# Sample rows projected with the first group of prompt tiles, their attention placed behind its routing; staging buffer in two halves

## The chip, the cores and the metric

One core of a Trainium2 chip runs one launch of a Bass/Tile kernel. The metric is device microseconds of that launch, as a median of a few executions. Arithmetic is float32 throughout; in the last stage float32 operands are split in a high and a low part. Instructions run on five engines, each in its own fixed order: PE (matrix products), DVE (vector), ACT (scalar, activations), POOL (here only the indirect row gathers) and SP (issues nearly all other transfers). The order on each engine is decided when the program is built, by the Tile framework's scheduler from its own estimates; at run time nothing overtakes.

## The reference, cut

One layer of a hybrid decoder for 1024 prompt rows and 8 sample rows with the same weights:

```python
h = rmsnorm(x) * (1 + sc1) + sh1
qa, ka, va, ub, vb, xr, xg = split(h @ w_in)            # 1024 -> 2560 columns
ya = dilated attention(q, k, v)       # sample rows: against their cache of 512 rows and themselves
yb = spatial_gate(ub, rmsnorm(vb));   yc = rglru_block(xr, xg)
x = x + g1 * ([rms(ya) | rms(yb) | rms(yc)] @ w_out)
x = x + g2 * peer_ffn(rmsnorm(x) * (1 + sc2) + sh2)
def peer_ffn(h):                      # 8 heads, 16 experts each, of 16384
    q = rmsnorm(h @ w_q); s = q . sub_keys              # 2 x 128 scores a head
    e, g = top 16 of the sums of the two top-16 lists;  g = softmax
    act = gelu(h . u_tab[e]);  return sum over k of (g * act)_k v_tab[e_k]
def dilated_attn_sample(q, k_all, v_all):   # three branches, merged by their denominators
    logits = q . k_all[idx] * scale + bias;  out = softmax(logits) . v_all[idx]
```

## The kernel before, in words

The prompt is eight tiles of 128 rows; the eight sample rows are tile `NT`. The kernel has a **front** and a **last stage**, and a **gather stream** runs beside both.

The front goes over `GROUPS` = (0,1), (2,3), (4,5,NT), (6,7). For each group `project` loads the five 512-column blocks of `w_in` (L86, four transfers a block, a ring of four buffers) and forms q, k, v and the two other mixers; `mix_and_route` does the attention of its prompt tiles (L605 scores, L622 values), for `NT` calls `sample_attention`, then multiplies by `w_out` (into L696), normalises, multiplies by `w_q`, and takes the top-16 lists. `select` turns these into 128 expert numbers and gates a row. A product of a prompt tile is eight matmuls (L237); of `NT` it is eight narrow ones and a summing one (L241, L245).

Tiles 1, 3, 4, 5 (`DENSE`) are later multiplied with all 16384 experts, and for that `gate_table` writes their gates as a table to HBM: per step DVE makes one-hot rows (L796), four matmuls go to the single buffer `psG` (L804), and ACT copies it to `st` (L805); every fourth step one 1 MB transfer writes `st` out (L806, `g_d<-st`). `st` has one buffer. The steps are fed into the program between attention heads (`pump`).

Tiles 0, 2, 6, 7 (`GATHER`) and at last `NT` go through the gather stream (`experts`): POOL fetches 128 rows of `peer_u`, one a partition, 512 KB a time (L893), DVE forms the dot product (L901), 128 times; then the same with `peer_v` and a weighted sum (L910). Tiles follow each other strictly: 256 gathers, then L917 and L918 finish the tile, its output leaves, and the next tile's rows are loaded into the same buffer `gx`. `NT` needs 8 + 8 gathers. The ring `grow` has five buffers, so POOL runs at most five gathers ahead of DVE.

The last stage `dense` starts when all gate tables are written: 128 blocks of `peer_u` and `peer_v` are loaded and split (L969), multiplied (L999 scores, L1015 values), and added up on DVE (L1024); it ends with L1043 and L1044 for each dense tile.

`sample_attention` takes for each of the 8 sequences the row q (`qb`), two blocks of cached keys (`kc`: 128 and 96 rows), multiplies and sums on DVE (L824, L825), forms the softmax, and multiplies with two blocks of cached values each (`vc`, L868, 16 matmuls into one `psv`). Its tiles come from the routing stream's ring `R.a2`, four buffers; two of them hold the weights `pz` while the values come in.

Of the kernel before, what the change touches and what calls it, by code (L numbers as in the profile page):

```python
# [21 lines left out]
D = 1024  # L22
NT = 8
GATHER = (0, 2, 6, 7)
DENSE = (1, 3, 4, 5)
GROUPS = ((0, 1), (2, 3), (4, 5, NT), (6, 7))
# [33 lines left out]
def kernel(ctx: ExitStack, tc: tile.TileContext, I, O):  # L60
# [12 lines left out]
    class Stream:  # L73


        def __init__(self, key, weights, rows):
            self.key, self.weights, self.rows = key, weights, rows
# [4 lines left out]
        def load_w(self, src):  # L82
            ws = []
            for j in range(4):
                w = fr.tile([P, 2, 512], F32, tag="w" + self.key, name="w", bufs=self.weights)
# [13 lines left out]
    Z = Stream("z", 4, 4)  # L99
    R = Stream("r", 4, 4)  # L100
# [435 lines left out]
    qT, mix = {}, {}  # L536

    def project(grp):
# [7 lines left out]
        for nb in (4, 0, 1, 3, 2):  # L546
            w = Z.load_w(I["w_in"][nb])
            for t in grp:
# [79 lines left out]
    def mix_and_route(grp, first):  # L628
        if first:
            ada(R, "g1")  # L630
        pt = [t for t in grp if t < NT]
        sums = {t: sm.tile([P, 8], F32, tag="sums", name="sums", bufs=4) for t in pt}
# [20 lines left out]
        if NT in grp:  # L653
            sample_attention(mix[NT])
# [131 lines left out]

    def gate_table(t):
# [3 lines left out]
        for b in range(P // TB):  # L791
            st = fr.tile([P, P, TB], F32, tag="st", name="st", bufs=1)
            for n0 in range(0, TB, 4):
# [5 lines left out]
                ps = mm.tile([P, 512], F32, tag="pg", name="psG", bufs=BANKS["g"])  # L799
                for q in range(4):  # L800
# [9 lines left out]
    def sample_attention(mix):  # L810
# [7 lines left out]
        for b in range(8):  # L818
            qb = R.a2("qb")
            S.dma_start(qb, dram_ap(q_d, b * 512, [[0, P], [1, 512]]))  # L820
            for j, (r0, st, n) in enumerate(blk):
                kc = R.a2("kc")
# [3 lines left out]
        kn = R.a2("kn")[:8]  # L826
        S.dma_start(kn, k_d)
        qs = R.a2("qs2")[:8]
# [5 lines left out]
        lg = R.a2("lgs")[:64, :225]  # L834
# [5 lines left out]
        ohs = R.a2("ohs")[:33, :225]  # L840
# [16 lines left out]
        for j, n in ((0, P), (1, 96)):  # L857
            z = R.a2("pz").rearrange("p (b c) -> p b c", b=8)
# [4 lines left out]
        po = R.ps("psv")  # L863
        for b in range(8):
            for j, (r0, st, n) in enumerate(blk):
                vc = R.a2("vc")
# [7 lines left out]
        om = R.a2("om")[:64]  # L874
# [6 lines left out]
        tv_ = R.a2("tv")[:8]  # L881
# [3 lines left out]
        V.tensor_tensor(mix[:8, 0:512], tv_, py[:8], op=ALU.add)  # L885
# [290 lines left out]
```

## Time and profile before

| | us |
|---|---|
| median of 3 runs | 3316.39 (3306.85 to 3317.27) |
| profiled execution, whole | 3327.76 |
| its span, first to last instruction | 3326.0 |
| busy in the span: PE / DVE / POOL / ACT | 2795.2 / 2543.4 / 1394.1 / 1201.9 |

The profiled execution is 0.3% over the median, so sums are made against its span and carried over as a ratio. The busy shares are averages over stages of different kinds: the front (to about 1707 us), the last stage (to about 3314 us) and a short end.

### The profile page before, as it was taken

The numbers are of one execution on the slowest core, as the hardware profiler recorded it, in microseconds if no ns is written. First come the engines' busy times: TensorE is split into PE (matmuls) and PEld (weight loads), VectorE is DVE, ScalarE is ACT, GpSimd is POOL, SyncE is SP. The second block draws the span as 40 slices with busy tenths as digits, with TensorE's granted clock in tenths as the row PEclk, the third lists the DMA queues.
The fourth block names the chain that finished last, engine by engine and source line by source line (L and its number), as shares of the span: only waits on it lengthen the run. The fifth ranks groups of instructions, "written<-read, shape, count | busy, mean of one in ns | idle before, by whom it ended". The sixth has DMA issues, their size and how long they took to land.

```text
span 3326.0 us, 35751 instructions
## 1 busy us (share of the span) xinstructions
PE 2795.2 (84%) x11152; PEld 1879.5 (57%) x11152; DVE 2543.4 (76%) x5342; ACT 1201.9 (36%) x2583; POOL 1394.1 (42%) x1046
## 2 busy tenths in 40 slices
PE   7999976868944888976759998988989988989997
PEld 2444353423630333554437777777777776777776
DVE  1324876896675777876799898788898888898896
ACT  2453474443630342664543222222222222222221
POOL 0000043414235532034323565466566656566563
PEclk8999997987955999987879999999999999999998
DMA  7556677947787987478887999899999999999996
GB/s 276 179 195 198 217 250 269 335 170 287 221 253 247 352 261 285 139 229 296 276 287 252 347 333 334 301 345 339 348 329 342 344 344 342 360 332 333 346 347 218
DMA packets 340157, 952.56 MB, mean 286 GB/s; under 512 B 35063, under 2 KB 117550, under 8 KB 337918
## 3 DMA queue, kind: packets, MB, share of 16 engines
q0 software_dynamic: 149760, 545.33, 46.6%
q1 hardware_dynamic: 190206, 404.95, 35.1%
q8 instruction: 88, 1.44, 0.2%
q14 instruction: 103, 0.84, 0.1%
HBM read 894.04 MB, written 60.85 MB: 287 GB/s over the span
## 4 chain that ended last, share of the span: by engine, by line
PE 27%; DMA 23%; issue 20%; POOL 14%; DVE 12%; ACT 3%; SPq 0%; POOLq 0%; DVEq 0%; ACTq 0%
POOL grow L893 14%; PE psz L237 10%; DMA grow<-in_peer_v,ge 8%; DMA g_d<-st 5%; PE psG L804 3%; DVE grow L901 3%; DMA grow<-in_peer_u,ge 2%; PE pst L162 2%; PE pso L622 2%; PE psS L999 2%; PE psO L1015 2%; PE lg L605 2%; PE psa L194 2%; DVE acc L910 1%; DMA w<-in_w_in 1%
## 5 line engine op out<-in xcount | busy, mean ns | idle before, releaser
L893 POOL DMA_INDIRECT grow<-in_peer_u,ge x520 | 685.2, 1318 | 1333.2 <-DVE grow L901 540.5
L893 POOL DMA_INDIRECT grow<-in_peer_v,ge x520 | 708.3, 1362 | 565.7 <-DVE acc L910 359.2
L910 DVE SCALAR_TENSOR_TENSOR acc<-grow,dot,acc 128x1024 f32<-128x1024 f32 x515 | 660.1, 1282 | 136.6 <-DMA grow<-in_peer_v,ge 129.5
L237 PE MATMUL psz<-w,hT 128*128 128x512 f32 x1408 | 682.7, 617 | 59.4 <-DMA w<-in_w_in 28.4
L901 DVE SCALAR_TENSOR_TENSOR grow<-grow,gx 128x1024 f32<-128x1024 f32 x520 | 625.8, 1219 | 133.5 <-DMA grow<-in_peer_u,ge 108.9
L237 PEld LDWEIGHTS psz<-w,hT 128*128 128x128 f32 x1408 | 253.2, 196 | 324.1 <-issue 223.0
L1015 PE MATMUL psO<-vh,ah 128*128 128x512 f32 x512 | 223.2, 436 | 120.8 <-DVE acc L1024 120.3
L804 PE MATMUL psG<-o,oh 128*128 128x128 f32 x1024 | 205.8, 339 | 121.0 <-ACT st L805 113.3
L968 ACT CAST vh<-v 128x1024 fp32r<-128x1024 f32 x128 | 125.2, 1048 | 492.5 <-PE psO L1015 491.1
L804 PEld LDWEIGHTS psG<-o,oh 128*128 128x128 f32 x1024 | 170.9, 232 | 208.7 <-ACT st L805 147.8
L796 DVE TENSOR_TENSOR oh<-iof,tr 128x1024 f32<-128x1024 f32 x128 | 156.5, 1224 | 134.2 <-PE psG L804 129.5
L968 ACT CAST ah<-a 128x512 fp32r<-128x512 f32 x128 | 79.6, 622 | 398.0 <-DVE a L1004 398.0
L968 ACT CAST uh<-u 128x1024 fp32r<-128x1024 f32 x128 | 135.1, 1055 | 236.6 <-PE psS L999 236.4
L1015 PE MATMUL psO<-vl,ah 128*128 128x512 f32 x512 | 216.9, 424 | 0.0
L1015 PE MATMUL psO<-vh,al 128*128 128x512 f32 x512 | 215.2, 420 | 0.0
L803 ACT ACTIVATE o<-oh,tr 128x128 f32<-128x128 f32 x512 | 185.5, 397 | 53.2 <-PE psG L804 44.0
L1015 PE MATMUL psK<-vh,al 128*128 128x512 f32 x512 | 199.9, 391 | 5.0 <-DVE al L969 5.0
L1015 PE MATMUL psK<-vh,ah 128*128 128x512 f32 x512 | 200.0, 391 | 2.3 <-ACT ah L968 2.3
L1015 PE MATMUL psK<-vl,ah 128*128 128x512 f32 x512 | 199.8, 390 | 0.0
L1015 PEld LDWEIGHTS psO<-vh,ah 128*128 128x128 f32 x512 | 107.2, 209 | 159.8 <-DVE acc L1024 136.3
L969 DVE TENSOR_TENSOR ul<-u,uh 128x1024 fp32r<-128x1024 f32 x128 | 156.1, 1220 | 5.5 <-ACT uh L968 5.5
L969 DVE TENSOR_TENSOR vl<-v,vh 128x1024 fp32r<-128x1024 f32 x128 | 150.6, 1219 | 0.5 <-ACT vh L968 0.4
(370 smaller groups left out, 5002.8 us busy)
## 6 DMA issues: line engine op xcount, KB each, us to landing
u<-in_peer_uT SPq DMA_DIRECT2D x128, 512.0 KB
v<-in_peer_v SPq DMA_DIRECT2D x128, 512.0 KB
w<-in_w_in SPq DMA_DIRECT2D x80, 512.0 KB
w<-in_wq SPq DMA_DIRECT2D x64, 512.0 KB
g_d<-st SPq DMA_DIRECT2D x32, 1024.0 KB
gc<-g_d SPq DMA_DIRECT2D x16, 2048.0 KB
w<-in_w_ada SPq DMA_DIRECT2D x48, 512.0 KB
w<-in_w_out SPq DMA_DIRECT2D x32, 512.0 KB
```

What stands on the lines that cost most here:

```text
L162: T.transpose(pv[:, c, :r], src[:, (c0 + c) * P:(c0 + c + 1) * P], ident[:r, :r])
L194: T.matmul(ps[32 * j:32 * j + 32, :], sc[:, 2 * j + kk, :], w(2 * j + kk), start=(kk == 0), stop=(kk == 1 and j > 0))
L237: T.matmul(ps, xT[:, c, :], w(c), start=(c == 0), stop=(c == 7))
L796: V.tensor_tensor(oh, iof[:, None, None, :].to_broadcast([P, 2, OHB, P]), tt[:, 0:2, b * TB + n0:b * TB + n0 + OHB, None].to_broadcast([P, ...
L803: A.activation(o1, oh[:, 0, n0 % OHB + q, :], AF.Copy, scale=tt[:, 2, n:n + 1])
L804: T.matmul(ps[:, q * P:(q + 1) * P], oh[:, 1, n0 % OHB + q, :], o1, start=True, stop=True)
L893: G.indirect_dma_start(out=rt, out_offset=None, in_=tab, in_offset=bass.IndirectOffsetOnAxis(ap=idx, axis=0))
L901: V.scalar_tensor_tensor(rt, rt, 1.0, x, op0=ALU.mult, op1=ALU.mult, accum_out=w[:, k:k + 1])
L910: V.scalar_tensor_tensor(acc, rt, w[:, k:k + 1], acc, op0=ALU.mult, op1=ALU.add)
L968: A.copy(hi, x)
L969: eng.tensor_tensor(lo, x, hi, op=ALU.subtract)
L1015: T.matmul(ps, aa[x][:, t * P:(t + 1) * P], vv[y][:, hf * 512:(hf + 1) * 512], start=(k == 0 and (first or o not in keep)), stop=(k == 3 * ...
```

## The change

The sample rows move from the third group to the first one in `project` (`PROJECT`), and to the second one in `mix_and_route` (`GROUPS`). `sample_attention` stands by itself, right behind the routing of the first group; it hands its result over by a small HBM tensor `mix_d`. Its tiles no longer come from `R.a2` but from the buffers of the gate table: alternately `st`, which is now two halves with two buffers, and `oh12` (class `Early`). Its value product takes the buffer of `psG`. `gate_table` copies each step in two halves and writes two 512 KB transfers. `select` of a gather tile follows its routing at once, where it came after the next group's projection; `select(NT)` keeps that place. The modulation row `g2` is formed one group later.

```diff
-GROUPS = ((0, 1), (2, 3), (4, 5, NT), (6, 7))
+PROJECT = ((0, 1, NT), (2, 3), (4, 5), (6, 7))
+GROUPS = ((0, 1), (2, 3, NT), (4, 5), (6, 7))
...
+    class Early:
+
+        n = 0
+
+        def a2(self, name):
+            self.n += 1
+            shape, tag = (([P, P // 2, TB], "st"), ([P, 2, OHB, P], "oh12"))[self.n % 2]
+            x = fr.tile(shape, F32, tag=tag, name=name, bufs=2)
...
+        if NT in grp:
+            S.dma_start(mix_d[:, 512:1024], mix.pop(NT)[:8, 512:1024])
...
+        if NT in grp:
+            mix[NT] = fr.tile([P, D], F32, tag="mix", name="mix", bufs=4)
+            S.dma_start(mix[NT][:8], mix_d)
...
-        if NT in grp:
-            sample_attention(mix[NT])
...
-            st = fr.tile([P, P, TB], F32, tag="st", name="st", bufs=1)
+            sts = [fr.tile([P, P // 2, TB], F32, tag="st", name="st", bufs=2) for _ in range(2)]
...
-                A.copy(st[:, :, n0:n0 + 4], ps.rearrange("p (n c) -> p c n", n=4))
-            S.dma_start(g_d[:, :, j * (P // TB) + b, :, :].rearrange("g p c n -> p g (c n)"),
-                        st.rearrange("p (g c) n -> p g (c n)", c=GST))
+                for st, pv in zip(sts, ps.rearrange("p (n two c) -> two p c n", n=4, two=2)):
+                    A.copy(st[:, :, n0:n0 + 4], pv)
+            hg = P // GST // 2
+            for m, st in enumerate(sts):
+                S.dma_start(g_d[m * hg:(m + 1) * hg, :, j * (P // TB) + b, :, :].rearrange("g p c n -> p g (c n)"),
+                            st.rearrange("p (g c) n -> p g (c n)", c=GST))
...
-            qb = R.a2("qb")
+            qb = X.a2("qb")
...
-        po = R.ps("psv")
+        po = gate_ps("psv")
...
-        V.tensor_tensor(mix[:8, 0:512], tv_, py[:8], op=ALU.add)
+        V.tensor_tensor(tv_, tv_, py[:8], op=ALU.add)
+        S.dma_start(mix_d[:, 0:512], tv_)
...
     for i, grp in enumerate(GROUPS):
-        project(grp)
+        project(PROJECT[i])
         while late:
             now(select(late.pop()))
         mix_and_route(grp, i == 0)
...
             if t in DENSE:
                 pending += [select(t), gate_table(t)]
+            elif t == NT:
+                late.append(t)
             else:
-                late.append(t)
+                now(select(t))
         if i == 0:
+            sample_attention()
+        if i == 1:
             ada(R, "g2")
```

The order on the engines moves as follows. On PE, the sample attention (`psl`, `psb`, `psv`) of before stands between the last gate-table matmuls of the third group's attention and that group's first transposes of `mix`, with nothing of other work between its rows:

```order
L804 MATMUL psG<-o_6088,oh_6076 128x128
L837 MATMUL psl<-ident,lgT_6299 64x128
L838 MATMUL psl<-ident,lgT_6300 64x96
L843 MATMUL psb<-ohs,rb 64x225
L855 MATMUL psl<-ident,lgs 128x64
L856 MATMUL psl<-ident,lgs 96x64
L868 MATMUL psv<-vc,pz 64x512 x16
L878 MATMUL psv<-om,bm 8x512
L162 MATMUL pst<-ident,mix 128x128 x16
```

In the changed kernel (its own line numbers: L249 is the product `psz`, L174 a transpose, L493 a mixer) the same rows stand in the projection of the second group, a part of them is shown:

```order
L859 MATMUL psl<-ident,lgT_2324 64x128
L860 MATMUL psl<-ident,lgT_2325 64x96
L249 MATMUL psz<-w,hT 128x512
L865 MATMUL psb<-ohs,rb 64x225
L249 MATMUL psz<-w,hT 128x512 x12
L877 MATMUL psl<-ident,lgs 128x64
L878 MATMUL psl<-ident,lgs 96x64
L249 MATMUL psz<-w,hT 128x512 x4
L890 MATMUL psv<-vc,pz 64x512 x2
L174 MATMUL pst<-ident,z 128x128 x4
L890 MATMUL psv<-vc,pz 64x512 x2
L249 MATMUL psz<-w,hT 128x512 x2
```

Between the first and the last of the 16 value products (`psv`) stand now 17 products of the second group's projection and 8 transposes, which do not depend on them. On SP, the projection of the first group loads its weights (`w<-in_w_in`) like this in the kernel before:

```order
L86 DMA w<-in_w_in 128x1024 x6
L580 DMA out_k_p<-z 128x512
L583 DMA kT_d<-kt 128x4x128
L86 DMA w<-in_w_in 128x1024 x2
L580 DMA out_k_p<-z 128x512
L583 DMA kT_d<-kt 128x4x128
L640 DMA kT<-kT_d 128x256
L86 DMA w<-in_w_in 128x1024 x4
```

and in the changed kernel (L87 is the weights, L842 and L845 are the queries and cached keys of the sample rows) like this:

```order
L581 DMA q_d<-z 8x512
L842 DMA qb<-q_d 128x512
L845 DMA kc<-in_cache_k 96x512
L842 DMA qb<-q_d 128x512
L593 DMA out_k_p<-z 128x512
L845 DMA kc<-in_cache_k 96x512
L596 DMA kT_d<-kt 128x4x128
L845 DMA kc<-in_cache_k 128x512
L842 DMA qb<-q_d 128x512
L87 DMA w<-in_w_in 128x1024 x3
L593 DMA out_k_p<-z 128x512
L596 DMA kT_d<-kt 128x4x128
```

The weights now stand behind sample loads, each of which needs a free one of four buffers. On DVE, the program ends like this before (L910 with `dot` is the last gathers of the sample rows, L1024 to L1044 the end of the last stage, L947 the last step of the sample rows):

```order
L910 SCALAR_TENSOR_TENSOR acc<-grow,dot,acc 128x1024
L1044 TENSOR_TENSOR x1f<-x1f,tmp 128x1024
L1024 TENSOR_TENSOR acc_10713<-acc_10713,psO 128x512
L1043 TENSOR_TENSOR tmp<-grw,acc_10713 128x512
...
L1024 TENSOR_TENSOR acc_10716<-acc_10716,psO 128x512
L1043 TENSOR_TENSOR tmp<-grw,acc_10716 128x512
L1044 TENSOR_TENSOR x1f<-x1f,tmp 128x1024
L947 TENSOR_REDUCE fin<-part 128x64
```

and like this in the changed kernel, whose L933, L924 and L1067 are L910, L901 and L1044 of before:

```order
L933 SCALAR_TENSOR_TENSOR acc<-grow,dot,acc 128x1024
L1067 TENSOR_TENSOR x1f<-x1f,tmp 128x1024
L933 SCALAR_TENSOR_TENSOR acc<-grow,dot,acc 128x1024 x19
L940 TENSOR_TENSOR acc<-acc,grw 128x1024
L941 TENSOR_TENSOR acc<-acc,x1f 128x1024
L924 SCALAR_TENSOR_TENSOR grow,dot<-grow,gx 128x1024 x8
L926 TENSOR_TENSOR dot<-dot,gw 128x8
L931 TENSOR_SCALAR acc<-grow,dot 128x1024
L933 SCALAR_TENSOR_TENSOR acc<-grow,dot,acc 128x1024 x7
L973 TENSOR_REDUCE fin<-part 128x64
```

Behind the last row of the last stage stand now 19 sums of tile 7 and all of the sample rows' experts. Counted over DVE's whole order, 372 of the 1040 gather rows (L901, L908, L910) stand ahead of the first split of the last stage before, and 323 in the changed kernel; between that split and the last row L1044 there are 668 before, and 682 in the changed kernel. Apart from these 49 rows, what stands ahead of the last stage is the same set of instructions on PE and DVE; ACT has 128 copies of `st` and 7 table loads more there, SP 35 transfers more.

## Rows read from the trace of the kernel before

**Rows 1.** Busy time by stretch: stretch, its length, busy us (count) by engine.

```profile
core 0: us, PE busy (x) PEld busy (x) DVE busy (x) ACT busy (x) POOL busy (x), PEclk, DMA share, GB/s
0.00:396.00 396.00, 369.05 (x1210) 156.87 (x1210) 156.47 (x788) 158.90 (x407) 0.63 (x6) 0.97 0.63 211
396.00:767.00 371.00, 279.12 (x1081) 152.38 (x1081) 292.98 (x964) 196.24 (x498) 130.99 (x103) 0.86 0.73 252
767.00:976.00 209.00, 158.82 (x683) 102.72 (x679) 141.68 (x238) 111.74 (x275) 70.86 (x55) 0.74 0.80 259
976.00:1082.00 106.00, 34.66 (x42) 5.58 (x42) 63.95 (x75) 9.51 (x43) 56.70 (x41) 0.52 0.81 251
...
1707.00:3314.00 1607.00, 1456.59 (x6144) 1186.90 (x6144) 1397.45 (x1801) 420.69 (x537) 914.28 (x663) 0.95 0.91 329
3314.00:3326.00 12.00, 0.00 (x0) 0.00 (x0) 2.32 (x4) 0.00 (x0) 0.00 (x0) 0.56 0.34 85
```

**Rows 2.** PE's timeline, sample attention: start, length, what, idle and releaser.

```profile
974.04 2.08 PE L804 MATMUL psG<-o,oh 128*128 128x128 f32 x8 [0.68 <-ACT st L805]
...
1081.84 1.97 PE L162 MATMUL pst<-ident,mix 128*128 128x128 f32 x8 [8.10 <-ACT mix L669]
```

**Rows 3.** Who waited for whom, 976 to 1084 us: total us, times, longest.

```profile
ACT junk L666 <- PE psv L868: 62.1, 1, 62.1
```

**Rows 4.** Chain of waits, first and last transfer of cached values: start, length.

```profile
1016.40 8.25 DMA vc<-in_cache_v
...
1066.39 2.64 DMA vc<-in_cache_v
```

**Rows 5.** Groups of PE instructions, 60 to 396 us (each product is recorded as two).

```profile
L237 PE MATMUL psz<-w,hT 128*128 128x512 f32 x507 | 234.5, 602 | 5.3 <-DMA w<-in_w_in 4.8 <-DVE hT L327 0.5
```

**Rows 6.** What SP's queue waited for, 900 to 1085 us.

```profile
SPq L867 <- PE psv L868: 24.1, 13, 2.1
SPq L823 <- DVE lgT L825: 24.1, 7, 10.1
SPq L867 <- DMA vc<-in_cache_v: 18.8, 9, 5.9
```

**Rows 7.** ACT copies from PSUM (ns min/median/max), table loads in one stretch.

```profile
L805 ACT COPY st<-psG x128: 563/586/595, 425.1 to 1657.1; 128x512 f32<-128x512 f32 x128
...
L534 ACT COPY mix<-psy x8: 373/377/378, 87.0 to 1223.0; 128x256 f32<-128x256 f32 x8
...
L148 ACT ACT_TABLE_LOAD x4 | 5.1, 1283 | 0.1
```

**Rows 8.** Who waited for whom, whole span.

```profile
POOL grow L893 <- issue: 159.1, 520, 0.9
PEld psG L804 <- ACT st L805: 147.8, 81, 10.6
...
ACT st L805 <- DMA g_d<-st: 114.9, 24, 16.0
```

**Rows 9.** The page's costliest groups, the gather stream's: busy, mean ns | idle before.

```profile
L893 POOL DMA_INDIRECT grow<-in_peer_v,ge x520 | 708.3, 1362 | 565.7 <-DVE acc L910 359.2
L910 DVE SCALAR_TENSOR_TENSOR acc<-grow,dot,acc 128x1024 f32<-128x1024 f32 x515 | 660.1, 1282 | 136.6 <-DMA grow<-in_peer_v,ge 129.5
...
L901 DVE SCALAR_TENSOR_TENSOR grow<-grow,gx 128x1024 f32<-128x1024 f32 x520 | 625.8, 1219 | 133.5 <-DMA grow<-in_peer_u,ge 108.9
```

**Rows 10.** Timeline of DVE near the end.

```profile
3269.15 1.23 DVE L901 SCALAR_TENSOR_TENSOR grow<-grow,gx 128x1024 f32<-128x1024 f32 x1 [7.21 <-DMA gx<-h_d]
...
3301.06 1.28 DVE L910 SCALAR_TENSOR_TENSOR acc<-grow,dot,acc 128x1024 f32<-128x1024 f32 x1
...
3312.78 1.23 DVE L1044 TENSOR_TENSOR x1f<-x1f,tmp 128x1024 f32<-128x1024 f32 x1
```

**Rows 11.** Chain of waits behind the end of tile 7.

```profile
3256.66 5.92 DMA out_xp<-acc
3262.59 6.46 DMA gx<-h_d
```

More of the change, by code (lines that the diff above doesn't have):

```diff
@@ L73, with __init__ @@
     class Stream:
-        def __init__(self, key, weights, rows):
-            self.key, self.weights, self.rows = key, weights, rows
+        def __init__(self, key, rows):
+            self.key, self.rows = key, rows
         def ps(self, name="ps", kind="s"):
@@ L84, in load_w @@
             for j in range(4):
-                w = fr.tile([P, 2, 512], F32, tag="w" + self.key, name="w", bufs=self.weights)
+                w = fr.tile([P, 2, 512], F32, tag="w" + self.key, name="w", bufs=4)
                 S.dma_start(w, src[j])
@@ L97, in small @@
             return sm.tile([P, n], F32, tag=f"{nm}{n}{self.key}", name=nm, bufs=bufs)
-    Z = Stream("z", 4, 4)
-    R = Stream("r", 4, 4)
+    Z = Stream("z", 4)
+    R = Stream("r", 4)
+    class Early:
[4 more added lines that the diff above has]
+            x = fr.tile(shape, F32, tag=tag, name=name, bufs=2)
+            return x.rearrange("p a b -> p (a b)")[:, :512] if tag == "st" else x.rearrange("p a b c -> p (a b c)")[:, :512]
+    X = Early()
     def a4(name):
@@ L536 @@
     qT, mix = {}, {}
+    mix_d = dpool.tile([8, D], F32, name="mix_d")
     def project(grp):
@@ L785, in select, with gate_ps @@
         A.copy(tr[t], ps[:, :3 * P].rearrange("p (q n) -> p q n", q=3))
+    def gate_ps(name):
+        return mm.tile([P, 512], F32, tag="pg", name=name, bufs=BANKS["g"])
     def gate_table(t):
@@ L798, in gate_table @@
                                     op=ALU.is_equal)
-                ps = mm.tile([P, 512], F32, tag="pg", name="psG", bufs=BANKS["g"])
+                ps = gate_ps("psG")
                 for q in range(4):
@@ L804, in gate_table, with sample_attention @@
                     T.matmul(ps[:, q * P:(q + 1) * P], oh[:, 1, n0 % OHB + q, :], o1, start=True, stop=True)
-                A.copy(st[:, :, n0:n0 + 4], ps.rearrange("p (n c) -> p c n", n=4))
-            S.dma_start(g_d[:, :, j * (P // TB) + b, :, :].rearrange("g p c n -> p g (c n)"),
-                        st.rearrange("p (g c) n -> p g (c n)", c=GST))
+                for st, pv in zip(sts, ps.rearrange("p (n two c) -> two p c n", n=4, two=2)):
[4 more added lines that the diff above has]
+                            st.rearrange("p (g c) n -> p g (c n)", c=GST))
             yield
-    def sample_attention(mix):
+    def sample_attention():
         n_d = dpool.tile([8, 8], F32, name="n_d")
@@ L818, in sample_attention @@
         for b in range(8):
-            qb = R.a2("qb")
+            qb = X.a2("qb")
             S.dma_start(qb, dram_ap(q_d, b * 512, [[0, P], [1, 512]]))
             for j, (r0, st, n) in enumerate(blk):
-                kc = R.a2("kc")
+                kc = X.a2("kc")
                 S.dma_start(kc[:n], dram_ap(I["cache_k"], (b * 512 + r0) * 512, [[512 * st, n], [1, 512]]))
@@ L825, in sample_attention @@
                 V.tensor_reduce(lgT[j][:n, b, :], kc[:n].rearrange("p (h e) -> p h e", h=8), axis=AX.X, op=ALU.add)
-        kn = R.a2("kn")[:8]
+        kn = X.a2("kn")[:8]
         S.dma_start(kn, k_d)
-        qs = R.a2("qs2")[:8]
+        qs = X.a2("qs2")[:8]
         S.dma_start(qs, q_d)
@@ L833, in sample_attention @@
         S.dma_start(n_d, ln)
-        lg = R.a2("lgs")[:64, :225]
+        lg = X.a2("lgs")[:64, :225]
         S.dma_start(lg[:, 224:225], dram_ap(n_d, 0, [[1, 64], [1, 1]]))
@@ L839, in sample_attention @@
         A.copy(lg[:, 0:224], ps[:64, 0:224])
-        ohs = R.a2("ohs")[:33, :225]
+        ohs = X.a2("ohs")[:33, :225]
         S.dma_start(ohs, I["ohs"])
@@ L857, in sample_attention @@
         for j, n in ((0, P), (1, 96)):
-            z = R.a2("pz").rearrange("p (b c) -> p b c", b=8)
+            z = X.a2("pz").rearrange("p (b c) -> p b c", b=8)
             V.memset(z, 0.0)
@@ L862, in sample_attention @@
             pz.append(z)
-        po = R.ps("psv")
+        po = gate_ps("psv")
         for b in range(8):
             for j, (r0, st, n) in enumerate(blk):
-                vc = R.a2("vc")
+                vc = X.a2("vc")
                 S.dma_start(vc[:n], dram_ap(I["cache_v"], (b * 512 + r0) * 512, [[512 * st, n], [1, 512]]))
@@ L873, in sample_attention @@
         V.tensor_reduce(bm, ident[:64, :64].rearrange("p (b h) -> p b h", b=8), axis=AX.X, op=ALU.add)
-        om = R.a2("om")[:64]
+        om = X.a2("om")[:64]
         V.tensor_tensor(om.rearrange("p (h e) -> p h e", h=8), po[:64].rearrange("p (h e) -> p h e", h=8),
@@ L880, in sample_attention @@
         S.dma_start(pn, dram_ap(p_d, 0, [[8, 8], [1, 8]]))
-        tv_ = R.a2("tv")[:8]
+        tv_ = X.a2("tv")[:8]
         S.dma_start(tv_, v_d)
```

## Prediction

> **What bounds the kernel now.** I first cut the span into its stages. The front lasts to 1707 us, the last stage from there to 3314 us, and 12 us follow [rows 1]. In the last stage everything is near full at once: in 1607 us PE is busy 1457, DVE 1397, and the transfer engines 0.91 of the time. No single engine is the bound there, and the order on DVE, in which the dense work and the gather stream are woven together, fixes the pace. The first 396 us are PE's: busy 369 of 396 at a granted clock of 0.97, with DVE at 156. In between lies one stretch in which PE does almost nothing: from 976 to 1082 us it is busy 34.7 of 106 us, at a clock of 0.52 [rows 1]. That is the sample attention. The timeline of PE shows it between the last gate-table matmul and the first transpose of `mix` [rows 2], and the waits name who stands still: ACT waits 62.1 us in one piece for `psv`, since the norm of `mix` of the group stands behind it [rows 3]. The gather stream goes on meanwhile (POOL busy 56.7 of the 106 us), so that the stretch is dead for the front but not for the whole kernel. This is the point on which the forecast turns.
>
> **The change part by part.** The work is conserved, as the counts in the section on the change say, so I follow the idle time of PE through the front, and then the end.
>
> *The dead stretch goes.* It has 106 − 34.7 = 71 us without PE, and the sample products in it ran at a granted clock of 0.52. Where they stand now the clock was 0.97 [rows 1], about its upper level (2.4 GHz) instead of the lower one (1.2), so 34.7 us become some 18. Together −88 us in the front.
>
> *What waits where the sample rows stand now.* The 16 loads of cached values took from 1016 to 1069 us, 53 us [rows 4], with two free buffers, as now. Between the first and the last of their products stand now 17 products of 0.93 us (two records of 234.5/507 us, [rows 5]), 16 of the sample rows at the same price, and a few small ones: some 35 us of cover. If the loads keep their pace, 18 us are bare; without gathers beside them (POOL has none before 396 us, [rows 1]) they should be quicker. The other place is SP. The queries and keys stand ahead of weights, and SP stops at each that has no free buffer. In the present kernel SP waited 24.1 + 24.1 + 18.8 us for such buffers and values [rows 6]. The weight ring hides part: when one of the four tiles comes free, three are still to be used, 3 x 4 x 0.93 = 11 us of products for two prompt tiles. I take +15 us for both, from 0 (all covered) to 67 (every SP wait becomes a wait of PE). Queued behind them are the projections of the first two groups, and with these the start of the gathers.
>
> *The staging in halves.* A copy of 512 columns takes 586 ns, one of 256 from PSUM 377 [rows 7]; two are 168 ns dearer, 21.5 us for 128 steps. It is on the path where PE waits for the copy, 81 of the 128 steps [rows 8]: +14 us (0 to 22). The 7 more table loads of 1.28 us [rows 7] are 9 us on an engine that is busy 36%: +3 (0 to 9). The wait for the transfer itself, 114.9 us in 24 pieces [rows 8], I leave as it is: both halves are sent behind the last of the four steps, and `psG` has one buffer, so the next matmuls wait until the second half has landed too.
>
> *Less gather work in the front.* 49 dot products of 1.22 us [rows 9], 60 us of DVE, move out of the front. Some of them were what the front waited for; I take −15 us (0 to −60).
>
> *Early select.* Nothing for tile 2: its gathers follow those of tile 0 on POOL, and by 976 us, in the third group's attention, only 103 + 55 of tile 0's 256 were issued [rows 1]. Nothing for tile 0 either, as long as its lists come no earlier; the longer first part rather delays them.
>
> So the last stage starts at −88 + 15 + 14 + 3 − 15 = **−71 us**.
>
> *The last stage* has 682 gather rows beside it instead of 668: 14 × 1.28 us = 18 us of DVE [rows 9], of which I count half, since DVE is busy 87% of the time there (0 to 18). In exchange the change of buffers from tile 7 to the sample rows leaves it, which now stops DVE for 7.2 us [rows 10] and holds rows of the last blocks behind it: −10 (0 to −20). Together −1.
>
> *The end* pays. Before, the last dense row ended at 3314 us [rows 10] and only 12 us followed [rows 1]. Now 19 sums of tile 7 and the whole of the sample rows' experts follow. Up to four gathers are there already (4 × 1.28 us), the other 15 come at POOL's own pace of 1.36 + 0.31 us between two [rows 8, 9]: 30 us. Finishing the tile takes two DVE rows (2.4), its output and the next `gx` 5.9 + 6.5 us [rows 11], eight dot products 9.8, eight sums 10.3, and what came behind the last sum took from 3302 to 3326 us [rows 10]; without dense transfers ahead of it on SP I take 20 of these 24. Sum 85 us against 12: **+73 us** (60 to 90).
>
> Total: −71 − 1 + 73 = +1, so 3327 us on the span, 3326 × 1.0003. In the scale of the runs shown (the profiled span is 0.3% over their median): 3317, rounded to **3316 us**. The dead stretch is worth its 88 us to the front, and nearly the same is given back, because the gathers that filled it now stand alone at the end.
>
> **The rivals.** *B, the front gains more (faster).* The dots that leave the front count in full (60 instead of 15 us), or a step may start when the first half of `st` is out, which would save up to half of the 114.9 us [rows 8], 57 us. Either gives 3327 − 45 to 3327 − 57 = 3270 to 3282 on the span, 3260 to 3272 in the runs' scale. For it: DVE was busy 293 of 371 us between 396 and 767 us [rows 1]. Against the half: the single buffer `psG`. A rule of the Trainium skill (Perfetto Trace Analysis, DMA Optimizations) speaks for the half: splitting a transfer into smaller ones may let the whole end sooner where the transfer engines are mostly idle. Another one of the Trainium skill (DMA: Bandwidth & Descriptors, Rules for kernel authors) speaks against it: for bandwidth it wants 1 MiB or more in a DMA, and it calls two transfers to disjoint partition halves (here they are halves of the columns) not worth it, because they serialize. The trace has only whole transfers here, so no run shows which holds; the sum stays as it is by the second and would be 57 us lower by the first.
>
> *C, SP holds the weights back (slower).* Every wait of SP for a sample buffer reaches PE, 67 us instead of 15: 3327 + 52 = 3379 on the span, 3369 in the runs' scale. It decides from the point where the waits exceed the 11 us that the ring hides per block. For it: in the shown piece of SP's order three weight tiles stand behind eight sample and output transfers. Against: PE waited only 4.8 us for weights between 60 and 396 us [rows 5], and the transfer engines were busy only 0.63 of that time [rows 1].
>
> *D, no effect at all beyond the order*: the gather stream, the one chain that runs through front and last stage, keeps its mean pace whatever stands beside it, and the time changes only with its start. It starts as now, or 18 + 15 = 33 us later behind the longer first part: 3326 to 3359 on the span, 3316 to 3349 in the runs' scale.
>
> **How the numbers follow.** A measurement of this kernel can tell about 0.3%, 10 us, from no change. A, the sum, has 0.46; its own spread is about ±25 us (3291 to 3341), of which a half lies within 10 us: 0.12 faster, 0.22 same, 0.12 slower. B has 0.27, C 0.19, D 0.08 (0.02 faster, 0.02 same, 0.04 slower). Faster 0.12 + 0.27 + 0.02 = 0.41; same 0.24; slower 0.12 + 0.19 + 0.04 = 0.35. The range reaches half way and more into B and C: 3266 to 3362.
>
> **What would show it.** In the profile after: no stretch with PE under 40% between 400 and 1600 us; the first split of the last stage (the x rows of L969's successor) at about 1636 us; the last L1044's successor 71 or 72 us earlier than 3314, and some 85 us behind it in which PE is idle. Copies of `st` of about 377 ns, the waits for `g_d` unchanged near 115 us. C would show as waits of PE for `w<-in_w_in` well over 5 us before 400 us; B as a front below 1600 us. The prediction is wrong at its root if the last stage does not keep its 1607 us.

## The result, and the profile after

The changed kernel takes 3289.76 us (median), the one before 3316.83 us beside it: a ratio of 0.9898, with a 95% interval of 0.9856 to 0.994. One execution of the changed kernel took 5677 us, and is left out. A second comparison, beside the experiments, gave 0.9912 (0.9884 to 0.9941). So it is about 1% faster. The forecast's sum was no change (3316, range 3266 to 3362); of its three outcomes it gave faster the largest chance, 0.41.

The profiled execution after has a span of 3297.3 us, 28.7 less than the 3326.0 of before. Lines of the changed kernel have new numbers: L804 is now L823 (`psG`), L805 is L825 (copies to `st`), L868 is L890 (`psv`), L867 is L889 (loads of `vc`), L901 and L910 are L924 and L933 (dots and sums of the gather stream), L1044 is L1067 (last dense row).

The table by stretch, in the columns of [rows 1]; rows 2 to 4 are cut at the first attention products of the second, third and last group, the first is the place of the sample attention's value products (its key products ran on DVE from 136 to 194 us):

```profile
core 0: us, PE busy (x) PEld busy (x) DVE busy (x) ACT busy (x) POOL busy (x), PEclk, DMA share, GB/s
396.00:466.00 70.00, 54.04 (x124) 18.73 (x124) 54.23 (x230) 19.79 (x46) 11.64 (x11) 0.93 0.64 212
466.00:878.00 412.00, 339.74 (x1252) 171.88 (x1251) 314.22 (x997) 204.93 (x582) 176.91 (x132) 0.88 0.84 289
878.00:1225.00 347.00, 298.01 (x1154) 168.64 (x1155) 278.24 (x780) 191.42 (x515) 123.90 (x93) 0.91 0.79 269
1225.00:1592.00 367.00, 285.22 (x1286) 183.45 (x1284) 283.48 (x734) 210.39 (x617) 123.90 (x93) 0.85 0.74 248
1592.00:3209.00 1617.00, 1454.45 (x6144) 1185.40 (x6144) 1408.67 (x1855) 420.24 (x537) 935.83 (x682) 0.94 0.92 332
3209.00:3297.00 88.00, 0.00 (x0) 0.00 (x0) 48.46 (x49) 0.21 (x1) 39.89 (x31) 0.50 0.68 228
```

The row from 878 us is the third group, which held the dead stretch: it is now 347 us long. Before, between the same two marks (767 and 1338 us), it took 571. The second group's stretch grew from 372 to 412 us, the first one, up to the second group's first attention product, from 395 to 466. The last stage starts at 1592 us instead of 1707 and is 1617 us long instead of 1607, a difference no larger than its scatter (11 us, below). Behind the last dense row follow 88 us without one matmul, where there were 12. In short: **115 us won in the front, 10 lost in the last stage, 77 at the end**, together the 28.

The waits of the changed kernel that answer to [rows 8], over the whole span:

```profile
PEld psG L823 <- ACT st L825: 106.7, 74, 10.3
ACT st L825 <- DMA g_d<-st: 81.4, 37, 9.8
```

and its groups of PE for the attention's 32 products, and of ACT for the copies of `st` (busy us, mean ns, idle before):

```profile
L890 PE MATMUL psv<-vc,pz 128*64 128x512 f32 x16 | 9.4, 675 | 8.4 <-DMA vc<-in_cache_v 8.4
L890 PE MATMUL psv<-vc,pz 96*64 96x512 f32 x16 | 9.0, 646 | 3.6 <-DMA vc<-in_cache_v 2.6 <-ACT ny L160 1.0
...
L825 ACT COPY st<-psG 128x256 f32<-128x256 f32 x256 | 85.2, 373 | 120.3 <-DMA g_d<-st 81.4 <-PE psG L823 38.4
```

The 62.1 us in one piece of [rows 3] is gone. The attention's products wait 12 us in sum for their cached values and are busy 18 us.

The end of the changed kernel, in DVE's timeline:

```profile
3207.57 1.22 DVE L1067 TENSOR_TENSOR x1f<-x1f,tmp 128x1024 f32<-128x1024 f32 x1
...
3240.66 1.28 DVE L933 SCALAR_TENSOR_TENSOR acc<-grow,dot,acc 128x1024 f32<-128x1024 f32 x1 [1.39 <-DMA grow<-in_peer_v,ge]
3241.98 1.23 DVE L940 TENSOR_TENSOR acc<-acc,grw 128x1024 f32<-128x1024 f32 x1
3243.24 1.22 DVE L941 TENSOR_TENSOR acc<-acc,x1f 128x1024 f32<-128x1024 f32 x1
3257.67 1.23 DVE L924 SCALAR_TENSOR_TENSOR grow<-grow,gx 128x1024 f32<-128x1024 f32 x1 [13.21 <-DMA gx<-h_d]
...
3281.82 1.28 DVE L933 SCALAR_TENSOR_TENSOR acc<-grow,dot,acc 128x1024 f32<-128x1024 f32 x1 [0.28 <-DMA grow<-in_peer_v,ge]
3292.38 1.86 DVE L970 TENSOR_REDUCE fin<-part 128x64 f32<-128x1024 f32 x1 [9.27 <-DMA fin<-x_d]
```

The reader sees the two chains that the forecast set behind the last dense row: the last sums of tile 7 to 3241.9 us, then the two rows that finish the tile, 13.2 us until `gx` is there, the eight dots and eight sums of the sample rows, and their way through DRAM.

### The profile page after: what moved, and what is told of

Read it like the earlier page. It is cut to its first block, busy times and chain, and to the rows that moved or that the text cites. A ratio compares the mean times of both kernels' runs of the same rounds, so it can differ in the third digit from the quotient of the medians.

```text
span 3297.3 us, 35948 instructions
## 1 busy us (share of the span) xinstructions
PE 2775.9 (84%) x11152; PEld 1877.4 (57%) x11152; DVE 2543.4 (77%) x5342; ACT 1213.0 (37%) x2718; POOL 1412.7 (43%) x1046
## 4 chain that ended last, share of the span: by engine, by line
PE 26%; DMA 23%; issue 21%; POOL 16%; DVE 10%; ACT 4%; SPq 0%; POOLq 0%; DVEq 0%; ACTq 0%
POOL grow L916 16%; PE psz L249 10%; DMA grow<-in_peer_v,ge 9%; DMA g_d<-st 5%; PE psG L823 4%; PE pst L174 2%; PE pso L637 2%; PE lg L620 2%; DMA w<-in_w_in 1%; DVE grow L924 1%; PE psa L206 1%; DVE acc L933 1%; DMA grow<-in_peer_u,ge 1%; DMA w<-in_wq 1%; PE psS L1022 1%
## 5 line engine op out<-in xcount | busy, mean ns | idle before, releaser
L916 POOL DMA_INDIRECT grow<-in_peer_u,ge x520 | 699.2, 1345 | 1146.8 <-DVE grow L924 466.5
L933 DVE SCALAR_TENSOR_TENSOR acc<-grow,dot,acc 128x1024 f32<-128x1024 f32 x515 | 659.8, 1281 | 121.8 <-DMA grow<-in_peer_v,ge 115.0
L249 PE MATMUL psz<-w,hT 128*128 128x512 f32 x1408 | 699.3, 629 | 61.7 <-DMA w<-in_w_in 22.4
L924 DVE SCALAR_TENSOR_TENSOR grow<-grow,gx 128x1024 f32<-128x1024 f32 x520 | 626.1, 1219 | 152.9 <-DMA grow<-in_peer_u,ge 120.0
L249 PEld LDWEIGHTS psz<-w,hT 128*128 128x128 f32 x1408 | 257.6, 200 | 325.8 <-issue 228.3
L823 PEld LDWEIGHTS psG<-o,oh 128*128 128x128 f32 x1024 | 162.5, 220 | 168.3 <-ACT st L825 106.7
L823 PE MATMUL psG<-o,oh 128*128 128x128 f32 x1024 | 195.0, 323 | 74.9 <-ACT st L825 70.0
```

Source lines behind the costliest of these rows:

```text
L249: T.matmul(ps, xT[:, c, :], w(c), start=(c == 0), stop=(c == 7))
L823: T.matmul(ps[:, q * P:(q + 1) * P], oh[:, 1, n0 % OHB + q, :], o1, start=True, stop=True)
L916: G.indirect_dma_start(out=rt, out_offset=None, in_=tab, in_offset=bass.IndirectOffsetOnAxis(ap=idx, axis=0))
L924: V.scalar_tensor_tensor(rt, rt, 1.0, x, op0=ALU.mult, op1=ALU.mult, accum_out=w[:, k:k + 1])
L933: V.scalar_tensor_tensor(acc, rt, w[:, k:k + 1], acc, op0=ALU.mult, op1=ALU.add)
```

## The experiments

The intervals are 0.2 to 0.4% on either side. The lengths come from one profiled execution each: front up to the first dense split, last stage to the end of the last dense row, end behind it; "behind" counts the gather rows (dots and sums on DVE) that stand behind the last dense row. Two kernels were profiled twice, and tell the scatter: the front repeats within 3 us, the end within 2, the last stage only within 11.

| run | ratio (95%) | span | front | last stage | end | behind |
|---|---|---|---|---|---|---|
| before | 1 | 3326.0 | 1707 | 1607 | 12 | 0 |
| changed | 0.9898 (0.9856–0.994) | 3297.3 | 1592 | 1617 | 88 | 34 |
| e12, changed again | 0.9912 (0.9884–0.9941) | 3289.3 | 1592 | 1611 | 87 | 34 |
| e1, halves alone | 1.0045 (1.0025–1.0066) | 3338.4 | 1714 | 1620 | 4 | 0 |
| e2, late select | 0.9835 (0.9807–0.9863) | 3264.9 | 1608 | 1608 | 48 | 16 |
| e11, e2 again | 0.9857 (0.9826–0.9888) | 3272.3 | 1605 | 1619 | 48 | 16 |
| e3, samples third | 0.9929 (0.99–0.9957) | 3306.6 | 1597 | 1603 | 108 | 60 |
| e4, before, no attention | 0.9796 (0.9764–0.9827) | 3244.7 | 1550 | 1605 | 89 | 34 |
| e5, changed, no attention | 0.9816 (0.9782–0.985) | 3259.1 | 1566 | 1603 | 90 | 34 |
| e6, loads on POOL | 0.9885 (0.9851–0.9919) | 3273.0 | 1584 | 1593 | 97 | 40 |
| e7, routed with third | 0.9942 (0.9916–0.9967) | 3289.0 | 1562 | 1626 | 102 | 43 |
| e8, projected with second | 0.9986 (0.9965–1.0008) | 3312.3 | 1621 | 1606 | 85 | 33 |
| e9, before, second group | 1.0016 (0.9997–1.0035) | 3340.4 | 1726 | 1610 | 4 | 0 |
| e10, e2 with loads on POOL | 0.9891 (0.9863–0.992) | 3286.9 | 1612 | 1625 | 50 | 16 |

**e1: the kernel before with the staging in halves, and nothing else.**

```
-                A.copy(st[:, :, n0:n0 + 4], ps.rearrange("p (n c) -> p c n", n=4))
+                for st, pv in zip(sts, ps.rearrange("p (n two c) -> two p c n", n=4, two=2)):
+                    A.copy(st[:, :, n0:n0 + 4], pv)
```

> The kernel before with one part of the change: st in two halves with two buffers, two copies a step, two transfers of 512 KB. Theory H (the halves shorten the staging): the waits of PE for copies into st (L804's psG, 113.3 us before, 70.0 in the changed kernel) fall to 60 to 85 us, the waits of ACT for g_d from 114.9 to about 80, the front ends 25 to 45 us earlier, and the time is 0.985 to 0.994 of before. Theory C (the staging waits less only because the sample rows and their gathers no longer stand beside it): the waits stay at 105 to 125 us, the dearer copies cost up to 14 us, and the time is 0.999 to 1.005 of before.

The front is 7 us longer, the ratio 1.0045: alone, the halves lose. The edit also moved the order on DVE: 384 gather rows run in the front instead of 372, so the 7 us can't be put down to the copies alone. The groups and waits of ACT show both sides:

```profile
L809 ACT COPY st<-psG 128x256 f32<-128x256 f32 x256 | 85.3, 373 | 135.5 <-DMA g_d<-st 94.5 <-PE psG L807 40.7
```

The wait for the transfers falls from 114.9 to 94.5 us, and the copies are busy 85.3 us instead of 74.8 (twice as many, and 373 ns instead of 584). PE's weight loads still wait 130.6 us for the copies, 147.8 before [rows 8]. So the wait of ACT is shorter with the halves, but the front is not. The Trainium skill's sentence on splitting transfers (Perfetto Trace Analysis, DMA Optimizations) is for DMA engines that are generally idle; here they were busy 0.73 to 0.81 of the time from 396 to 1082 us [rows 1]. The 57 us that B had from the half did not come.

**e4: the kernel before without the sample attention**, the value rows standing in its place, so that its time is no time of the whole computation.

```
-            sample_attention(mix[NT])
+            S.dma_start(mix[NT][:8, 0:512], v_d)
```

> The kernel before without the attention of the sample rows (their v rows are taken in its place), nothing else changed. It gives the price of the dead stretch where it stood. Theory P (the stretch is worth its 88 us to the front, and the gathers that filled it come back at the end): front 1610 to 1630 us, an end of 80 to 90 us, time 0.993 to 1.000 of before. Rival M (it is worth more, since it also held the gate table's last steps and its loads stood among others): front 1560 to 1600 us, time 0.982 to 0.992 of before.

The front falls by 157 us to 1550, more than either theory had. All of it, but 5 us, comes from the third group's stretch, 571 us before and 419 now. The row of this stretch in e4:

```profile
767.00:1186.00 419.00, 358.92 (x1391) 187.09 (x1391) 325.25 (x877) 212.32 (x569) 177.59 (x139) 0.91 0.84 293
```

and in the kernel before, with the 76 us just ahead of the dead stretch, as a piece of it:

```profile
767.00:1338.00 571.00, 410.79 (x1435) 203.29 (x1431) 403.21 (x982) 216.56 (x586) 230.43 (x181) 0.79 0.82 273
900.00:976.00 76.00, 45.20 (x207) 37.86 (x207) 55.23 (x62) 41.22 (x103) 22.59 (x16) 0.60 0.87 257
```

PE is idle 60 us instead of 160, and 52 us less busy, at a granted clock of 0.91 instead of 0.79. The dead stretch of 106 us is only two thirds of the 152. The attention had begun before it, on SP and DVE: its key loads (L823) were issued from 914.8 us on, and its key products (L824) run from 923.9 us:

```profile
L823 SPq DMA_DIRECT2D kc<-in_cache_k x16: 327/332/1817, 914.8 to 979.4; - x16
L824 DVE TENSOR_TENSOR kc<-kc,qb x16: 675/686/693, 923.9 to 985.2; 128x512 f32<-128x512 f32 x8, 96x512 f32<-96x512 f32 x8
```

All that while PE had only the gate table to do: from 920.6 to 976 us its timeline has only matmuls of `psG`, with waits for `st` between them like these, and the granted clock over the 76 us from 900 was 0.60:

```profile
936.33 2.08 PE L804 MATMUL psG<-o,oh 128*128 128x128 f32 x8 [5.38 <-ACT st L805]
...
951.33 2.08 PE L804 MATMUL psG<-o,oh 128*128 128x128 f32 x8 [4.64 <-ACT st L805]
...
968.52 2.08 PE L804 MATMUL psG<-o,oh 128*128 128x128 f32 x8 [6.84 <-ACT st L805]
```

So what the attention holds up is measured better from the last product of the prompt tiles' attention (L650) to the first transpose of `mix`, which waits for the norm. Before, the first of these two is

```profile
915.83 1.09 PE L650 MATMUL psq<-ident,qT 128*128 128x128 f32 x8
```

and the second stands at 1081.84 us [rows 2], 166 us later. In e4 there are 25 us between them:

```profile
909.12 1.09 PE L650 MATMUL psq<-ident,qT 128*128 128x128 f32 x8
...
934.36 1.06 PE L162 MATMUL pst<-ident,mix 128*128 128x128 f32 x4
```

These 141 us are nearly all of the 152. In e4 the gate table is alone on PE for some 20 us (914 to 934), and its further steps stand between other products. The third group of the changed kernel has 26 us between the same two rows (997.74 to 1023.62).

**e5: the changed kernel without the sample attention**, in the same way.

```
-            sample_attention()
+            S.dma_start(mix_d[:, 0:512], v_d)
```

> The changed kernel with the sample attention left out (the first 512 columns of the sample rows of mix are taken from the value rows instead), so its time is no time of the whole computation. Theory M (the attention costs little in its new place; what the front gained came from taking it out of the third group's stretch): the first segment, 466 us long, becomes about 440 us, the front about 1565 us, the end stays at 80 to 90 us: 3265 us, ratio 0.985. Rival W (the 71 us that the first segment grew by are waits of the attention, since its loads and those of the weights stand on one queue): the first segment falls back below 420 us, the front to about 1545 us, ratio below 0.982. Rival N (the first segment is longer for the samples' projection alone, and the attention is hidden): first segment 460 us or more, ratio 0.99.

The front falls by 26 us (1592 to 1566), 22 of them in the first stretch, 466 to 444 us. So in its new place the attention costs 26 us, in the old one 157. The rest of the 71 us by which the first stretch grew, 49 us, is the samples' projection, since e5 still has it.

**e9: the kernel before with the sample rows in the second group**, one number changed.

```
-GROUPS = ((0, 1), (2, 3), (4, 5, NT), (6, 7))
+GROUPS = ((0, 1), (2, 3, NT), (4, 5), (6, 7))
```

> The kernel before with one number changed: the sample rows are projected, mixed and routed with the second group instead of the third, the attention still directly ahead of the norm of mix that waits for it. Theory P (what counts is the place of the attention relative to the norm that waits for it): a stretch of some 150 us beyond its own products now stands in the second group instead of the third, the front is as long as before (1707 us within 25), and the ratio is 0.995 to 1.01. Rival E (what counts is that the samples are done early, away from the third group's gathers): the front falls by 60 us or more and the ratio is 0.985 or lower.

Being early is worth nothing. The front is 1726 us, the ratio 1.0016. The second group's stretch is now 535 us, the third one 366, and the wait of [rows 3] has moved with the samples, to the tenth the same:

```profile
ACT junk L666 <- PE psv L868: 62.1, 1, 62.1
```

Between the last attention product of the prompt tiles and the first transpose of `mix` there are again 167 us, in the second group now (570.41 to 737.45). As in e1, the order moved too: 384 gather rows stand in this front, 372 before. What the front of the changed kernel wins, it wins by taking the attention from ahead of the norm that waits for it.

**e2, e11 and e12: the early select.** e2 and e11 are the changed kernel with the select of the gather tiles where it was before, behind the next group's projection (that of the samples stands there in both); e12 is the changed kernel again, beside e11.

```
-            elif t == NT:
-                late.append(t)
             else:
-                now(select(t))
+                late.append(t)
```

> The changed kernel with the select of the gather tiles back behind the next group's projection. Theory N (early select does nothing, as predicted): the same as the changed kernel within 0.3%, 0.987 to 0.993 of before. Rival S (early select is what lets the front run freely): the front ends 15 to 30 us later than the changed kernel's 1592 us, and the time is 0.995 to 1.000 of before. In its order 344 gather rows stand ahead of the last stage on DVE (323 in the changed kernel) and 16 behind it (35), so that under N with a longer front the end should be some 25 us shorter.

> The kernel of e2 once more, on the same chip as the changed kernel and the two above, to tell ratios apart that differ by half a per cent: 0.9835 again within 0.004. If the early select is a cost of the changed kernel, it stays under e12 by 0.004 or more.

> The changed kernel itself beside e11: 0.9898 again within 0.004, above e11 by 0.004 or more if the early select costs something; equal to e11 if that difference was chance.

The early select is a loss: 0.9835 against 0.9898 in one comparison, 0.9857 against 0.9912 in the other, the same half per cent twice (15 us in the medians of the second, 3273.32 and 3288.51), though the intervals overlap by less than 0.001. In the second comparison every run of e11 (3256 to 3283 us) is shorter than every run of e12 (3284 to 3302). Both theories of e2 had its ratio higher. The same stretch of the front in the changed kernel, and then in e2:

```profile
465.00:873.00 408.00, 335.74 (x1243) 170.02 (x1242) 310.22 (x957) 204.93 (x582) 177.62 (x132) 0.88 0.84 290
```

```profile
465.00:873.00 408.00, 329.63 (x1250) 165.87 (x1248) 307.13 (x841) 198.84 (x578) 190.76 (x149) 0.91 0.88 313
```

DVE is as busy in both, but in the changed kernel with 116 instructions more and POOL with 17 gathers fewer. Over the whole front the early select has 323 gather rows where the late one has 344. It makes the front 13 to 16 us shorter, and 18 more rows stand behind the last dense row, which makes the end 39 to 40 us longer. DVE's timeline at the end of e2:

```profile
3215.47 1.23 DVE L1067 TENSOR_TENSOR x1f<-x1f,tmp 128x1024 f32<-128x1024 f32 x1 [3.19 <-DMA x1f<-x_d]
3225.08 1.23 DVE L924 SCALAR_TENSOR_TENSOR grow<-grow,gx 128x1024 f32<-128x1024 f32 x1 [8.38 <-DMA gx<-h_d]
```

Tile 7 is already done beside the dense rows, and one chain is left, that of the samples. This is the fastest of the kernels here that do the whole computation.

**e3: the sample rows' experts behind tile 2 in the gather stream**, ahead of tiles 6 and 7.

```
     for t in GATHER:
         peer_prompt(t)
-    peer_sample()
+        if t == 2:
+            peer_sample()
```

> The changed kernel with the sample rows' experts third in the gather stream, between tiles 2 and 6, not last. In the changed kernel 88 us follow the last dense row, of which some 50 us are the sample rows' chain (next gx, 8 + 8 gathers, the sum over HBM). Theory E (these 50 us are bare): 61 gathers of tile 7 follow the last stage instead of 35, at 1.7 us, but the sample chain is gone; the end is 60 to 120 us and the last stage up to 30 us shorter for 26 gather rows fewer: 0.978 to 0.988 of before. Rival (the transfers bound the whole, and the order of the stream changes nothing): 0.988 to 0.993, as the changed kernel.

No gain, and not the 0.978 to 0.988 of theory E: one chain instead of two at the end, but 60 rows in it, and 108 us. Its interval overlaps with the changed kernel's.

**e6 and e10: the attention's queries, keys and values loaded on POOL's queue**, in the changed kernel and in e2.

```
-                S.dma_start(vc[:n], dram_ap(I["cache_v"], (b * 512 + r0) * 512, [[512 * st, n], [1, 512]]))
+                G.dma_start(vc[:n], dram_ap(I["cache_v"], (b * 512 + r0) * 512, [[512 * st, n], [1, 512]]))
```

> The changed kernel, but with the queries, cached keys and cached values of the sample attention loaded on POOL's queue instead of SP's. If SP's waits for sample buffers hold back the weights of the first groups (rival C of the prediction, 13.2 + 8.6 us of such waits seen on SP), the first segment of 466 us becomes 20 us or more shorter, and the ratio to the kernel before 0.983. If SP hides them behind the four weight tiles, the first segment changes by less than 5 us and the ratio stays at 0.99. A loss would show that POOL, which issues the first gathers at 442 us, is now held by the sample buffers instead.

> The late select of e2 and the loads on POOL's queue of e6 together. As e6 showed no shorter first segment, the same as e2: ratio 0.980 to 0.987, the end at 45 to 50 us with 16 rows behind the last dense row. If the last stage of 1593 us in e6 was the loads' doing and not chance, it is 1595 us again here and the ratio 0.977.

The first stretch is 473 us in e6 instead of 466, the ratio 0.9885: SP's place in the queue did not hold the weights back. The short last stage of e6 (1593) did not come again in e10 (1625), and e10, at 0.9891 beside the 0.9857 of e11 and above the 0.980 to 0.987 that was expected, is not faster than e2. Nothing shows that the loads made that last stage short; why e6 had it stays open.

**e7 and e8: two other places**, both with the late select. In e7 the samples are routed with the third group, all else as in e2; in e8 they are projected with the second group too, and their attention stands behind the second group's routing.

```
-GROUPS = ((0, 1), (2, 3, NT), (4, 5), (6, 7))
+GROUPS = ((0, 1), (2, 3), (4, 5, NT), (6, 7))
```

> The kernel with the late select of e2, and the sample rows routed with the third group again, while their projection and attention stay early. e2 and this one differ only in the group that routes the samples. If the gathers behind the last dense row set the end (theory of the prediction's last term), the gather work of the samples is the same in sum and the place of their routing moves only some 40 rows: 44 rows stand behind the last dense row here against 16 in e2, so the end is 25 us or more longer than the 48 us of e2, and the ratio 0.985 to 0.995. If what counts is that no group of three tiles stands early in the front, the front before the first dense row falls by more than 30 us and the ratio is below 0.98.

> Late select; the samples are projected with the second group, their attention stands behind the second group's routing, and they are routed with the third group. If the attention is cheap wherever it doesn't stand directly ahead of the norm that waits for it, the third segment is as short as in the changed kernel (about 350 to 420 us), the first one as short as before (about 400 us), gathers start at about 405 us, and the ratio is 0.975 to 0.985. If the attention needs PE to have prompt products beside it that do not depend on DVE's gathers (as in the first segment), the second or third segment grows by 50 us or more, and the ratio is 0.99 or above.

e7 has a front of 1562 us, 46 less than e2, and loses it again: 43 rows behind the last dense row instead of 16, an end of 102 us, a last stage of 1626. The end was seen right, and the lower front did not bring the ratio that the other theory tied to it. e8 fits neither theory: the gathers start at 402 us and the third stretch is 407 us, as the first had it, but the first stretch is 444 us instead of 400 and the ratio is 0.9986. Its front is still 86 us shorter than before; an end of 85 us (33 rows) takes nearly all of that back. Against e2 its third stretch is 41 us longer. e7, which routes the samples with the third group too, has 392 us there, 26 more than e2, so most of the 41 us came with the routing. Against e7 it is the second stretch, at the end of which e8's attention stands, that is longer: 398 us instead of 346. How much of these 52 us is the attention's was not settled; its products wait only 6.7 us for cached values.

## Why the prediction was right or wrong

The range held the time, by its width: the sum was 30 us too long on the span (3327 against 3297). The end was seen right, and the front gained 115 us instead of 71.

| term | forecast | measured | from |
|---|---|---|---|
| attention taken from the third group, with its dots | −106 − 15 = −121 | −157 | e4 against before |
| attention in the new place | 18 + 15 = +33 | +26 | e5 against changed |
| staging in halves, table loads | 14 + 3 = +17 | +7 | e1 against before |
| early select, earlier projection and routing | 0 | +9 | what is left |
| front | −71 | −115 | |
| last stage | −1 | +10, +4 | changed, e12 |
| end | +73 | +77 | |

The forecast's −88 for the dead stretch is split here in −106 and the 18 us of products that go elsewhere; e4, like the changed kernel, has 323 gather rows in the front instead of 372, so the 15 us for the dots belong into its row. The row of the halves comes from e1, whose front holds 12 gather rows more than that of before. The measured terms are differences of single profiled executions, and adding them up takes for granted that they don't act on each other.

**The step that failed is the size of the dead stretch.** I took it to be the 106 us in which PE stood nearly still, 976 to 1082, together with the dots 121 us. e4 shows 157. I had dated the attention by the stretch in which PE stood still, but it began on SP and DVE some 60 us earlier, with its key loads from 914.8 us on, and the norm of `mix` stood behind all of it: 166 us between the last product of the prompt tiles' attention and the first transpose of `mix`, against 25 in e4. In the first part of this PE worked on the gate table alone, and my row of 767 to 976 us [rows 1] averaged that with a busy stretch to a harmless 0.74. The mechanism (the norm of `mix` waits for the attention) was right, and e9 confirms it.

**The products and the clock.** That the moved products would run at the upper level was right. The rows of the tile's products give the shortest, median and longest one in ns, of before and then of the changed kernel:

```profile
L868 PE MATMUL psv<-vc,pz x32: 615/1061/1116, 1008.1 to 1070.0; 128*64 128x512 f32 x16, 96*64 96x512 f32 x16
```

```profile
L890 PE MATMUL psv<-vc,pz x32: 590/594/1085, 413.9 to 456.6; 128*64 128x512 f32 x16, 96*64 96x512 f32 x16
```

The median is 1061 ns in the dead stretch, where the granted clock was 0.52, about the lower level of 1.2 GHz [rows 1], and 594 ns now, in a stretch at 0.93, near the upper one of 2.4. The Trainium skill (Perfetto Trace Analysis, Matmul Optimizations) says that the matmul engine scales its power with its utilization, so that matmuls should execute back to back. The trace agrees as far as it goes: it shows the clock and not the power, and the two numbers above.

**The new place and rival C.** The forecast's +15 for what is bare, beside 18 us of products, came out as 26 in all. PE waited 5.5 us for `w_in` between 60 and 396 us, 4.8 before [rows 5], and SP waited 13.2 and 8.6 us for sample values and their buffers, and 6.1 for those of the keys. C is refuted, by these rows and by e6.

**The halves.** The price was too high (17 against 7 us in e1), and I left the wait for `g_d` as it was: it fell from 114.9 to 81.4 us, in e1 alone to 94.5. The longer way of B, up to 57 us from the earlier half, is refuted by e1. The Trainium skill's advice against two transfers to disjoint partition halves (DMA: Bandwidth & Descriptors, Rules for kernel authors) is not about halves of the columns, as here. e1's ratio agrees with it in the outcome; its reason, that they serialize, is not shown here, as the wait did fall.

**B came for another reason.** The front lies below 1600 us, the sign that I had named for B. What gives it is neither the half nor, as far as shown, the dots, but the larger price of the old place. Of the 49 gather rows that left the front 45 had run inside the 166 us in which the norm waited (53 rows there before, 8 between the same two marks in e4), and the chain of waits gives the gathers and their sums only some 8 us of these 166. No run takes the dots out alone, so their price stays open. e2, with 21 more rows and a front 13 to 16 us longer, would make it 32 to 38 us for 49 rows, but e2 moves the select as well, so this is an estimate, and part of the same −157.

**Early select at 0 was wrong.** I asked when the gathers of tile 2 could start, and not what the select displaces on DVE. It costs half a per cent.

**The end.** The sum of 85 us behind the last dense row was 88.5: the sums of tile 7 33 us (30), the tile's end 2.5 (2.4), output and `gx` 13.2 (12.4), the dots 12.3 (9.8), the sums of the samples 12.7 (10.3), the rest 14.2 (20).

**The other signs.** In no 50 us between 400 and 1600 us is PE under 40%; the lowest is 26.5 of 50, from 1550 to 1600. The copies of `st` take 373 ns (377). The last stage kept its length within its scatter. D is refuted: the first gather is issued 37 us later (442 instead of 405 us), and yet the kernel is faster.

## What to carry to other kernels

A stretch in which an engine stands still can cost more than its own length (here 152 us for 106), since the chain that causes it may have begun earlier on other engines: look for the chain's first load, and at the stretch just ahead in short windows and with the granted clock, before pricing it. Moving a long chain away from the instruction that waits for it was what shortened the front; moving it only earlier, with the waiting instruction still behind it, gave nothing. Where two streams share an order on one engine, count what an edit displaces from the slower stream into the end: here about 2.2 us for each row that fell behind the last dense one (48 us with 16 rows, 88 with 34), which took back two thirds of what the front had gained.

## What the runs showed that was not expected

The end grows with the number of gather rows behind the dense work almost as on a line, whichever edit put them there: 16 rows 48 to 50 us, 33 or 34 rows 85 to 90, 40 rows 97, 43 rows 102, and 60 rows 108 where only one chain is left (e3). A sum with no dense work beside it takes 1.28 us and comes every 1.8 us (19 from 3208.71 to 3240.66 us). The chain of waits of the changed kernel leads from there back to POOL's issues and the transfer:

```profile
3228.96 0.69 POOL grow L916
3229.65 0.64 issue
3230.28 1.86 POOL grow L916
3232.45 8.11 DMA grow<-in_peer_v,ge
3240.66 1.30 DVE acc L933
```

So here the stream, without company, still waits for its gathers to be issued and landed.

Moving the attention's 40 loads (8, 16 and 16) from SP's queue to POOL's, which issues all the gathers, changed nothing that can be measured (0.9885 against 0.9898), although POOL waited 19.6 us for the buffers of `vc` there:

```profile
POOL vc L889 <- PE psv L890: 19.6, 12, 5.5
```
